# Operand tiles moved to new SBUF places, and the one-hot operations of the dense expert weights issued one by one, in a two-layer fp32 transformer block on one core

## The chip, the cores and the metric

The kernel runs on one core of one Trainium2 chip. The metric is the device time of one execution in microseconds; the figure of a kernel is the median of its runs, and a profiled execution has a time of its own. Times inside the trace are counted from the first instruction of the profiled execution.

## The reference, cut to what matters

Two transformer layers run one after the other on 256 tokens of width 1024, everything in float32. The first layer computes three mixers (windowed attention, a bidirectional linear recurrence, attention over a memory), gates and sums them, and adds a feed-forward layer over 16384 tiny experts (`peer_ffn`): each token picks 8 x 16 of them by a product-key top-k, and

```
act = gelu(einsum('chkd,cd->chk', u_tab[ix], hx))
out = einsum('chk,chkd->cd', gx * act, v_tab[ix])
```

The second stack has an attention layer with a SwiGLU feed-forward, then an attention layer with forget gates and a mixture of 8 SwiGLU experts of which each token takes two.

## The kernel before, in words

**Arithmetic.** Each float32 operand of a large product is split into a high part (rounded to the type `float32r`) and a low part (the rest). A product is three matmuls: high x high, high x low, low x high. `mm_fm` (line 377) streams 256 columns of an activation (`XH`, `XL`) past a 128 x 128 block of weights that sits in the array; `mm_tm` (line 382) streams 512 columns of weights past a 128 x 128 block of activations. So the activations are the moving operand in the first form and the stationary one, brought in by a weight load, in the second. All matmuls are issued at line 375.

**Weights.** `Stream` carries all weight tiles in order. SyncE loads a tile of 128 x 1024 float32 into a raw buffer (line 186), ScalarE writes its high part (line 200), VectorE its low part (line 211, called the low part below). There are three pairs of high and low tiles, more in some stages; when a tile is taken, `ahead` first issues the low parts that are waiting and then loads and splits as far as buffers allow. In the routing, the dense expert stage and what follows it `st.lag` is set: the low part of a tile is issued when the next tile is taken.

**The dense expert stages.** The tiny experts are computed densely. `u_phase(half)` multiplies all 128 groups of 128 experts by the tokens, one weight tile per half-step, and applies GELU (ScalarE, lines 1268 to 1272; VectorE multiplies by the gate weights where they are known, line 1273). `g_phase` makes the dense gate weights: for 8 tokens at a time, `prep` builds one-hot tiles on VectorE with four operations (two comparisons, lines 1303 and 1304, two products, line 1307), 16 half-precision matmuls multiply them into `pg`, and lines 1327 and 1329 multiply or copy the result into `act`. `weave` runs `g_phase` beside `u_phase(1)`: after each half-step of `u_phase` it takes 1.56 steps of `g_phase`, where a step ends at a `yield`. A group of 8 tokens has three steps: both comparisons; both products; the matmuls with line 1327. `v_phase` then multiplies by `peer_v` in the 512-column form.

**The last stage** runs the 8 experts: `in_mm` and `out_mm` use the 512-column form with the weight tiles moving and `XH`/`XL`/`X2`/`aH`/`aL` stationary. Raw buffers there number 24.

**Places in SBUF.** Tiles lie where their pools put them; pools are stacks, one from the left and one from the right, and `pad` (line 352) allocates unused bytes. Counting the tile sizes up in the order of the code gives each tile's first byte; its remainder modulo 512 is called its place here. All offsets inside these tiles are multiples of 512 bytes, so one place holds for every operand of a tile. Before the change the places are:

| tiles | role | place |
|---|---|---|
| weights `hwb`, `lwb` (3 pairs) and `hwx`, `lwx` | weights | 128 |
| `hwm`, `lwm` (output projection of layer 1) | weights | 0 |
| `hwc`, `lwc` | weights | 256 |
| `hwd`, `lwd` | weights | 384 |
| `XH`, `XL` | activations, mostly 256-column form | 192 |
| `YH`, `YL` (the same buffers 64 bytes lower or higher) | activations, 512-column form | 128, 256 |
| `catH`, `catL` | activations | 320 |
| `mgH`/`mgL`, `cH`/`cL` of the first attention of layer 2, `gh`/`glo`, `X2H`/`X2L`, `aH`/`aL` | activations, 512-column form | 0 |
| `mh2`, `ml2` | activations | 448 |
| `xnH`/`xnL`, `dm0` | gather of tokens | 128, 192 |

Of the kernel before, what the change touches and what calls it, by code (L numbers as in the profile page):

```python
# [7 lines left out]
F32 = mybir.dt.float32  # L8
FR = mybir.dt.float32r
# [258 lines left out]
def weave(main, *sides):  # L268

    sides = [[s[0], s[1], s[2] if len(s) > 2 else 0, 0.0] for s in sides]  # L270
    for n, _ in enumerate(main):
        for s in sides:
            if n < s[2]:
                continue
            s[3] += s[1]
            while s[3] >= 1.0 and s[0] is not None:
                s[3] -= 1.0
                if next(s[0], "end") == "end":
                    s[0] = None
# [37 lines left out]
def program(ctx, tc, A, out, dbg=None, stop=None, force=False):  # L317
# [11 lines left out]
    def pool(stack, name, bufs=1, side=None):  # L329
        kw = {} if side is None else {"side": side}  # L330
        return stack.enter_context(tc.tile_pool(name=name, bufs=bufs, reuse_waits="tile", **kw))
# [7 lines left out]
    def psum_b(n, name):  # L339

        bank_b.close()
        return bank_b.enter_context(tc.tile_pool(name=name, bufs=n, space=PSUM))

    psb = [psum_b(4, "psb")]
    resid = pool(ctx, "resid")
    small = pool(ctx, "small", 3)
    x1d = ctx.enter_context(tc.tile_pool(name="dram", bufs=1, space=bass.MemoryType.DRAM)).tile([128, 2, D], F32, name="x1d")
    ctx.enter_context(tc.manual_schedule())

    st = Stream(nc, strm, 5, 3)  # L350

    def pad(p, nbytes):

        p.tile([128, nbytes // 4], F32, name=f"pad{nbytes}_{len(pads)}")
        pads.append(nbytes)

    pads = []

    def pa():
        return psum.tile([128, 512], F32, name="pa")  # L360
# [13 lines left out]
    def mm(p, a, b, s, e):  # L374
        E.matmul(p, a, b, start=s, stop=e)  # L375
# [6 lines left out]
    def mm_tm(p, h, l, xh, xl, s, e):  # L382
        mm(p, xh, h, s, False)
        mm(p, xh, l, False, False)
        mm(p, xl, h, False, e)
# [9 lines left out]
    def split_to(h, l, src):  # L395
        T.activation(h, src, AF.Copy)  # L396
        V.tensor_sub(l, src, h.bitcast(F32))  # L397
# [85 lines left out]
                yield  # L483

    xt = resid.tile([128, 2, D], F32, name="xt")


    xbuf = [resid.tile([128, 2064], FR, name="X" + c) for c in "HL"]

    def shifted(*o):  # L490
        return [b[:, n:n + 2048].rearrange("p (k t) -> p k t", k=8) for b, n in zip(xbuf, o)]

    XH, XL = shifted(16, 0)
    YH, YL = shifted(0, 16)
    pad(resid, 64)
    phr = Pools()
    ctx.push(lambda *e: phr.close())
    misc = pool(phr, "pmisc", side="right").tile([128, 2048], F32, name="misc")
    HS = [slice(0, 512), slice(512, 1024)]
# [332 lines left out]
    for m in range(NF):  # L832
        st.add("ffn", A["w_ffn"], 3 * m, 3 * m + 2)
        if m >= LAG:
            q = m - LAG
# [30 lines left out]
    with Pools() as pha:  # L866
        pA = pool(pha, "pA")
# [4 lines left out]
        km = misc[:, 0:1024].rearrange("p (m t) -> p m t", m=4)  # L872
        vm = misc[:, 1024:2048].rearrange("p (a b) -> p a b", a=2)
        mt = misc.rearrange("p (a b) -> p a b", a=2)
        pad(pA, 64)
        catH = pA.tile([128, 16, 256], FR, name="catH")
        catL = pA.tile([128, 16, 256], FR, name="catL")
        mh, ml = catH[:, 8:16], catL[:, 8:16]
# [217 lines left out]
        phase_end("mix")  # L1096

        p1 = pool(pha, "p1m")
        pad(p1, 32)
        mgH = p1.tile([128, 8, 256], FR, name="mgH")  # L1100
        mgL = p1.tile([128, 8, 256], FR, name="mgL")
        st.extend(p1, 1, 2, st.end("wo"), "m")

        def proj(mp):
# [33 lines left out]
    act = [None, pool(ph1, "pR", side="right").tile([128, 64, 256], F32, name="act1")]  # L1138
# [119 lines left out]
    def u_phase(half):  # L1258
        blk = Blocks("u")
        for k in range(0, 64, 2):  # L1260
            p = pa()
            for i in range(2):
                fm_tile(p[:, i * 256:i * 256 + 256], blk, 8, XH, XL)
                if i == 0:
                    yield
            n, pv, to = seen["t"], p.rearrange("p (k t) -> p k t", k=2), act[half][:, k:k + 2]
            if n == 0:
                T.activation(to, pv, AF.Gelu_apprx_tanh)
            else:
                T.activation(pv[:, :, :n], pv[:, :, :n], AF.Gelu_apprx_tanh)  # L1270
                if n < 256:
                    T.activation(to[:, :, n:], pv[:, :, n:], AF.Gelu_apprx_tanh)
                V.tensor_mul(to[:, :, :n], pv[:, :, :n], to[:, :, :n])
            seen["k"] += 2
            yield
# [18 lines left out]
    def g_phase(ps):  # L1294

        def prep(n):
            a, c = oha[n % 2], ohc[n % 2]

            def pairs(x, i):
                return x[:, i, n * 8:n * 8 + 8].rearrange("p (u j) -> p u j", j=2)[:, :, None].to_broadcast([128, 4, 128, 2])  # L1300

            keys = io2[:, None].to_broadcast([128, 4, 128, 2])
            V.tensor_tensor(c[:, 0], keys, pairs(ib, 0), op=OP.is_equal)
            V.tensor_tensor(a, keys, pairs(ib, 1), op=OP.is_equal)
            yield
            for i in (1, 0):
                V.tensor_tensor(c[:, i], c[:, 0], pairs(gp, i), op=OP.mult)
            yield

        yield from prep(0)  # L1310
        for n in range(32):
            if n < 31:
                yield from prep(n + 1)
            a, c = oha[n % 2], ohc[n % 2]
            p = ps.tile([128, 1024], F32, name="pg")
            for i in range(8):
                u, j = i // 2, i % 2
                for q in range(2):
                    mm(p[:, i * 128:i * 128 + 128], a[:, u, :, j], c[:, q, u, :, j], q == 0, q == 1)
            pv = p.rearrange("p (t k) -> p k t", t=8)  # L1320
            ts, K = slice(n * 8, n * 8 + 8), seen["k"]
            for half in range(2):
                lo, hi = half * 64, half * 64 + 64
                m = min(max(K, lo), hi)
                if m > lo:
                    v = act[half][:, :m - lo, ts]
                    V.scalar_tensor_tensor(v, pv[:, lo:m], 2.0 ** -15, v, op0=OP.mult, op1=OP.mult)
                if m < hi:
                    T.activation(act[half][:, m - lo:, ts], pv[:, m:hi], AF.Copy, scale=2.0 ** -15)
            seen["t"] += 8  # L1330
            yield

    vacc = []

    def v_parts(half):

        done = set()

        def need(k):
            for q in (k, k + 1):  # L1340
                if q < 32 and q not in done:
                    done.add(q)
                    s = (q % 4) * 2
                    split_to(YH[:, s:s + 2], YL[:, s:s + 2], act[half][:, q * 2:q * 2 + 2])
        return need

    def v_phase(half, R, after):
# [21 lines left out]
    def v_mm(half, k, t, h, l, ns=(0, 1)):  # L1369
        ts = slice(t * 128, t * 128 + 128)  # L1370
        for n in ns:
            mm_tm(vacc[t][n], h[:, HS[n]], l[:, HS[n]], YH[:, k % 8, ts], YL[:, k % 8, ts],
                  half == 0 and k == 0, half == 1 and k == 63)

    g = g_phase(psum_b(2, "psg"))
    weave(u_phase(1), (g, 1.56))
    run(g)
    psb[0] = psum_b(4, "psb2")
    dump("act0", act[0])
# [1 line left out]
    run(v_phase(0, 0, None))  # L1381
    ph0.close()

    st.extend(pool(ctx, "strmc"), 2, 1, len(st.items), "c")
    phd = Pools()
    ctx.push(lambda *e: phd.close())
    c3_ = pool(phd, "c3")
    phs = Pools()
    ctx.push(lambda *e: phs.close())
    st.extend(pool(phs, "strmd"), 0, 2, st.end("kv1v"), "d")  # L1390
    phm = Pools()
    ctx.push(lambda *e: phm.close())
    pm2 = pool(phm, "pm2")
# [10 lines left out]
    permb = load_const(c3_, "permb")  # L1404
    sink2 = c3_.tile([128, 12], F32, name="sink2")
    nc.gpsimd.dma_start(sink2, rows(A["sink2"], 12))
    pad(pm2, 64)
    mh2 = pm2.tile([128, 8, 256], FR, name="mh2")
    ml2 = pm2.tile([128, 8, 256], FR, name="ml2")
    pad(pm2, 64)  # L1410
    m2 = misc.rearrange("p (k t) -> p k t", k=8)
    nc.gpsimd.dma_start(m2, A["mem2"])

# [21 lines left out]
    pr = pool(ctx, "pr", side="right")  # L1435
# [45 lines left out]
    with Pools() as ph:  # L1481
        p2 = pool(ph, "p2")
        t2 = pool(ph, "t2", 2)
# [38 lines left out]
        for h in range(12):  # L1522
            b = (h % 2) * 64
# [19 lines left out]
    with Pools() as ph:  # L1543
        p2 = pool(ph, "p2", 2)
# [9 lines left out]
        for m in range(NF):  # L1554
            p = pa()
# [7 lines left out]
            if m >= LAG:  # L1563
                h, l = st.take("ffn")
# [11 lines left out]
    with Pools() as ph:  # L1576
        p2 = pool(ph, "p2")
        t2 = pool(ph, "t2", 2)
# [68 lines left out]
        for h in range(12):  # L1647
            b = (h % 2) * 64
# [29 lines left out]
    Mk = pr.tile([128, 2, 8], F32, name="Mk")  # L1678
    Gt = pr.tile([128, 2, 8], F32, name="Gt")
    pos = pr.tile([128, 2, 8], F32, name="pos")  # L1680
    xnH = pr.tile([128, 2, D], FR, name="xnH")
    xnL = pr.tile([128, 2, D], FR, name="xnL")

    pen = pr.tile([128, 2, 8], F32, name="pen")
    dm0 = pr.tile([128, 2, 256], FR, name="dm0")

    def one_hot(dm, e, t, off=0, n=2):
        for i in range(n):
# [83 lines left out]
    with Pools() as ph:  # L1772
        p2 = pool(ph, "p2", side="right")
        t2 = pool(ph, "t2", 2, side="right")
        pad(t2, 32)
        st.extend(pool(ph, "strm3"), 7, 0, len(st.items), "f")
        st.load()
        x2 = [p2.tile([128, 8, 128], FR, name="X2" + c) for c in "HL"]
# [1 line left out]
        def rows_of(e, n=1):  # L1780

            if e % 3 == 2:
                return x2
            o = e % 3 * 128
            return [X[:, :, o:o + n * 128] for X in (YH, YL)]
        cnt = p2.tile([128, 1], F32, name="cnt")
        cni = p2.tile([128, 1], I32, name="cni")
        pad(p2, 64)

        def gather(p, ks, dm):  # L1790

# [202 lines left out]
        b = [small.tile([128, 2, 6], F32, name="bn") for _ in range(2)]  # L1994
        for t in range(2):
            for n in range(2):
                d = way[e][0][:, t * 128:t * 128 + 128]
# [31 lines left out]
```

## Time and profile before

| | |
|---|---|
| median of 3 runs | 2421.37 us (2420.82 to 2423.57) |
| profiled execution | 2422.57 us, of which the span of instructions is 2420.8 us |
| TensorE (PE) | busy 2352.5 us, 97% |
| VectorE (DVE) | busy 1862.3 us, 77% |
| ScalarE (ACT) | busy 1406.0 us, 58% |
| weights read | 528.55 MB on SyncE's queue |

PE is the matmul row and PEld the weight load row. Consecutive matmuls overlap in the records: one begins while the one before it is still passing through the array. So what a matmul costs in a row of matmuls is the distance from its start to the next start, called the pitch below, and not its recorded duration; the duration is the pitch and a constant part, which is why "mean ns of one" in a grouped row still tells the state of a group. The middle stretches run in this order: attention and recurrence to 306 us, routing and `u_phase(0)` to 556, `u_phase(1)` with `g_phase` to 778, `v_phase` to about 1142, the two attention layers and the SwiGLU layer (1264 to 1448) to about 1600, the experts to 2400.

### The profile page before, as it was taken

The numbers are of one execution on the slowest core, as the hardware profiler recorded it, in microseconds if no ns is written. First come the engines' busy times: TensorE is split into PE (matmuls) and PEld (weight loads), VectorE is DVE, ScalarE is ACT, GpSimd is POOL, SyncE is SP. The second block draws the span as 40 slices with busy tenths as digits, with TensorE's granted clock in tenths as the row PEclk, the third lists the DMA queues.
The fourth block names the chain that finished last, engine by engine and source line by source line (L and its number), as shares of the span: only waits on it lengthen the run. The fifth ranks groups of instructions, "written<-read, shape, count | busy, mean of one in ns | idle before, by whom it ended". The sixth has DMA issues, their size and how long they took to land. (4 is left out here: it accounts for less than half of the span.)

```text
span 2420.8 us, 37592 instructions
## 1 busy us (share of the span) xinstructions
PE 2352.5 (97%) x14264; PEld 2040.6 (84%) x14264; DVE 1862.3 (77%) x2825; ACT 1406.0 (58%) x1920; POOL 35.2 (1%) x48
## 2 busy tenths in 40 slices
PE   9999999999999999999999999989899999999997
PEld 8988999999898888888879997778788888888885
DVE  7776569798888555656685567589889989999997
ACT  5684444444444445544545444458677877877875
POOL 0100000000000000000000000000000000000000
PEclk9999999999999999999999999989999999999999
DMA  7335455554444557654426544379899999999992
GB/s 271 114 129 184 167 194 173 178 180 151 144 141 165 192 191 247 209 190 157 149 92 230 184 158 165 104 286 370 300 335 355 365 337 348 369 346 341 363 356 82
DMA packets 149646, 545.53 MB, mean 225 GB/s; under 512 B 16960, under 2 KB 17088, under 8 KB 148816
## 3 DMA queue, kind: packets, MB, share of 16 engines
q1 hardware_dynamic: 145728, 528.55, 61.8%
q0 software_dynamic: 2720, 10.50, 1.4%
q10 hardware_dynamic: 1008, 4.00, 0.4%
q8 instruction: 114, 1.87, 0.3%
q14 instruction: 76, 0.62, 0.1%
HBM read 540.88 MB, written 2.10 MB: 224 GB/s over the span
## 5 line engine op out<-in xcount | busy, mean ns | idle before, releaser
L211 DVE TENSOR_TENSOR lwb<-rawb,hwb 128x1024 fp32r<-128x1024 f32 (+1 forms) x406 | 494.0, 1225 | 92.9 <-ACT hwb L200 90.8
L200 ACT ACTIVATE hwb<-rawb 128x1024 fp32r<-128x1024 f32 (+1 forms) x406 | 426.8, 1056 | 214.5 <-PE pb L375 88.1
L375 PE MATMUL pa<-XH,lwb 128*128 128x256 f32 x1848 | 505.3, 281 | 16.8 <-DVE lwb L211 16.1
L375 PE MATMUL pa<-XH,hwb 128*128 128x256 f32 x1848 | 509.1, 283 | 0.4 <-ACT XH L511 0.2
L375 PE MATMUL pa<-XL,hwb 128*128 128x256 f32 x1848 | 501.4, 279 | 0.0
L375 PEld LDWEIGHTS pa<-XH,lwb 128*128 128x128 f32 x1848 | 340.1, 187 | 24.6 <-DVE lwb L211 24.5
L375 PEld LDWEIGHTS pa<-XH,hwb 128*128 128x128 f32 x1848 | 340.8, 188 | 4.4 <-issue 1.3
L375 PEld LDWEIGHTS pa<-XL,hwb 128*128 128x128 f32 x1848 | 340.6, 188 | 1.1
L211 DVE TENSOR_TENSOR lwb<-rawe,hwb 128x1024 fp32r<-128x1024 f32 x176 | 210.9, 1222 | 24.0 <-ACT hwb L200 19.4
L200 ACT ACTIVATE hwb<-rawe 128x1024 fp32r<-128x1024 f32 x176 | 185.8, 1059 | 25.4 <-PE pb L375 11.6
L211 DVE TENSOR_TENSOR lwb<-rawf,hwb 128x1024 fp32r<-128x1024 f32 x130 | 156.6, 1222 | 17.8 <-ACT hwb L200 13.7
L375 PE MATMUL pb<-hwb,XL 128*128 128x512 f32 (+1 forms) x428 | 165.5, 387 | 0.1
L375 PE MATMUL pb<-lwb,XH 128*128 128x512 f32 (+1 forms) x428 | 165.0, 386 | 0.0
L375 PE MATMUL pb<-hwb,XH 128*128 128x512 f32 (+1 forms) x428 | 163.4, 382 | 1.2 <-ACT XH L396 1.2
L375 PE MATMUL pa<-hwb,XH 128*128 128x512 f32 x396 | 159.0, 401 | 0.0
L375 PE MATMUL pa<-hwb,XL 128*128 128x512 f32 x396 | 156.8, 396 | 0.0
L375 PE MATMUL pa<-lwb,XH 128*128 128x512 f32 x396 | 156.2, 395 | 0.0
L200 ACT ACTIVATE hwb<-rawf 128x1024 fp32r<-128x1024 f32 x130 | 137.1, 1059 | 23.2 <-PE pa L375 11.3
L397 DVE TENSOR_TENSOR XL<-act,XH 128x512 fp32r<-128x512 f32 x64 | 44.1, 691 | 109.3 <-ACT XH L396 109.3
L375 PE MATMUL pb<-hwb,aH 128*128 128x512 f32 x264 | 104.5, 396 | 0.0
L375 PE MATMUL pb<-lwb,aH 128*128 128x512 f32 x264 | 104.0, 394 | 0.0
L375 PE MATMUL pb<-hwb,aL 128*128 128x512 f32 x264 | 104.0, 394 | 0.0
(611 smaller groups left out, 4918.3 us busy)
## 6 DMA issues: line engine op xcount, KB each, us to landing
rawe<-w_e SPq DMA_DIRECT2D x220, 512.0 KB, 5.3
rawf<-w_e SPq DMA_DIRECT2D x152, 512.0 KB, 5.2
rawb<-w_u SPq DMA_DIRECT2D x128, 512.0 KB, 3.5
rawb<-w_e SPq DMA_DIRECT2D x112, 512.0 KB, 5.3
rawb<-w_vt SPq DMA_DIRECT2D x110, 512.0 KB, 4.3
rawb<-w_ffn SPq DMA_DIRECT2D x47, 512.0 KB, 4.8
rawc<-w_e SPq DMA_DIRECT2D x44, 512.0 KB, 5.2
rawb<-w_mrg SPq DMA_DIRECT2D x36, 512.0 KB, 3.8
```

Source lines behind the costliest of these rows:

```text
L200: self.nc.scalar.activation(h[:, :n], r[:, :n], AF.Copy)
L211: self.nc.vector.tensor_sub(l[:, :n], r[:, :n], h[:, :n].bitcast(F32))
L375: E.matmul(p, a, b, start=s, stop=e)
L397: V.tensor_sub(l, src, h.bitcast(F32))
```

## The change

Two things. In `prep`, each of the four one-hot operations ends a step of its own (5 steps for 8 tokens instead of 3), and `weave` takes 2.6 steps after each half-step instead of 1.56. And tiles move: pads are added, changed or dropped, `small` is opened before `resid`, and `XH`/`XL` become plain tiles that serve both forms (`YH`/`YL` are gone).

```diff
     psb = [psum_b(4, "psb")]
+    small = pool(ctx, "small", 3)
     resid = pool(ctx, "resid")
-    small = pool(ctx, "small", 3)
...
-    xbuf = [resid.tile([128, 2064], FR, name="X" + c) for c in "HL"]
-
-    def shifted(*o):
-        return [b[:, n:n + 2048].rearrange("p (k t) -> p k t", k=8) for b, n in zip(xbuf, o)]
-
-    XH, XL = shifted(16, 0)
-    YH, YL = shifted(0, 16)
-    pad(resid, 64)
+    XH = resid.tile([128, 8, 256], FR, name="XH")
+    XL = resid.tile([128, 8, 256], FR, name="XL")
...
-        pad(pA, 64)
         catH = pA.tile([128, 16, 256], FR, name="catH")
...
-        pad(p1, 32)
+        pad(p1, 352)
         mgH = p1.tile([128, 8, 256], FR, name="mgH")
         mgL = p1.tile([128, 8, 256], FR, name="mgL")
+        pad(p1, 64)
         st.extend(p1, 1, 2, st.end("wo"), "m")
...
             V.tensor_tensor(c[:, 0], keys, pairs(ib, 0), op=OP.is_equal)
+            yield
             V.tensor_tensor(a, keys, pairs(ib, 1), op=OP.is_equal)
             yield
             for i in (1, 0):
                 V.tensor_tensor(c[:, i], c[:, 0], pairs(gp, i), op=OP.mult)
-            yield
+                yield
...
-                    split_to(YH[:, s:s + 2], YL[:, s:s + 2], act[half][:, q * 2:q * 2 + 2])
+                    split_to(XH[:, s:s + 2], XL[:, s:s + 2], act[half][:, q * 2:q * 2 + 2])
...
-            mm_tm(vacc[t][n], h[:, HS[n]], l[:, HS[n]], YH[:, k % 8, ts], YL[:, k % 8, ts],
+            mm_tm(vacc[t][n], h[:, HS[n]], l[:, HS[n]], XH[:, k % 8, ts], XL[:, k % 8, ts],
...
-    weave(u_phase(1), (g, 1.56))
+    weave(u_phase(1), (g, 2.6))
...
-    st.extend(pool(ctx, "strmc"), 2, 1, len(st.items), "c")
+    strmc = pool(ctx, "strmc")
+    pad(strmc, 64)
+    st.extend(strmc, 2, 1, len(st.items), "c")
...
-    st.extend(pool(phs, "strmd"), 0, 2, st.end("kv1v"), "d")
+    strmd = pool(phs, "strmd")
+    pad(strmd, 384)
+    st.extend(strmd, 0, 2, st.end("kv1v"), "d")
...
-    pad(pm2, 64)
+    pad(pm2, 448)
     mh2 = pm2.tile([128, 8, 256], FR, name="mh2")
     ml2 = pm2.tile([128, 8, 256], FR, name="ml2")
-    pad(pm2, 64)
...
+    dm0 = pr.tile([128, 2, 256], FR, name="dm0")
+    pen = pr.tile([128, 2, 8], F32, name="pen")
     xnH = pr.tile([128, 2, D], FR, name="xnH")
     xnL = pr.tile([128, 2, D], FR, name="xnL")
-
-    pen = pr.tile([128, 2, 8], F32, name="pen")
-    dm0 = pr.tile([128, 2, 256], FR, name="dm0")
...
-        pad(t2, 32)
...
-            return [X[:, :, o:o + n * 128] for X in (YH, YL)]
+            return [X[:, :, o:o + n * 128] for X in (XH, XL)]
...
-        pad(p2, 64)
```

Counted up in the same way, the places after the change are 128 for all weight tiles, 64 for `XH`/`XL`, `cat`, `mg`, `mh2`/`ml2`, the first `cH`/`cL`, `gh`/`glo`, `X2` and `aH`/`aL`, 128 for `dm0` and 192 for `xnH`/`xnL`.

## Rows read from the trace of the kernel before

**Rows 1.** The page's first part: busy time, share and instructions of each engine.

```profile
PE 2352.5 (97%) x14264; PEld 2040.6 (84%) x14264; DVE 1862.3 (77%) x2825; ACT 1406.0 (58%) x1920; POOL 35.2 (1%) x48
```

**Rows 2.** Busy time by stretch: PE, PEld, DVE, ACT, POOL, then clock, DMA share, GB/s.

```profile
300.00:556.00 256.00, 253.20 (x2125) 249.85 (x2124) 217.98 (x557) 120.88 (x143) 1.07 (x2) 1.00 0.53 178
556.00:778.00 222.00, 208.46 (x1963) 201.96 (x1961) 186.71 (x274) 91.31 (x151) 0.53 (x1) 1.00 0.44 147
...
1804.00:2004.00 200.00, 200.00 (x910) 162.85 (x909) 184.25 (x207) 157.72 (x191) 0.00 (x0) 1.00 0.97 351
```

**Rows 3.** One of the page's costliest groups: x count | busy us, mean ns | idle before it.

```profile
L375 PE MATMUL pa<-XH,lwb 128*128 128x256 f32 x1848 | 505.3, 281 | 16.8 <-DVE lwb L211 16.1
```

**Rows 4.** PE by instruction, u_phase(0): first and last of 48 pitches (start us, us).

```profile
380.04 0.28 PE L375 MATMUL pa<-XH,hwb 128*128 128x256 f32 x1
...
385.69 0.28 PE L375 MATMUL pa<-XH,hwb 128*128 128x256 f32 x1
```

**Rows 5.** PE by instruction, SwiGLU layer, weights `hwc`: first and last of 21 pitches.

```profile
1275.98 0.28 PE L375 MATMUL pa<-XH,hwc 128*128 128x256 f32 x1
...
1278.36 0.28 PE L375 MATMUL pa<-XH,hwc 128*128 128x256 f32 x1
```

**Rows 6.** PE by instruction, u_phase(1): a wait, then first and last of 18 pitches.

```profile
606.48 0.38 PE L375 MATMUL pa<-XH,lwb 128*128 128x256 f32 x1
606.70 0.28 PE L375 MATMUL pa<-XH,hwb 128*128 128x256 f32 x1
...
608.74 0.28 PE L375 MATMUL pa<-XH,hwb 128*128 128x256 f32 x1
```

**Rows 7.** PE by instruction, value projection of layer 1: first and last of 18 pitches.

```profile
64.23 0.28 PE L375 MATMUL pb<-hwb,XH 128*128 128x256 f32 x1
...
66.35 0.28 PE L375 MATMUL pb<-hwb,XH 128*128 128x256 f32 x1
```

**Rows 8.** PE groups of 46 to 57 us, memory values of layer 1, 512-column form.

```profile
L375 PE MATMUL pb<-lwb,catH 128*128 128x512 f32 x16 | 6.3, 392 | 0.0
L375 PE MATMUL pb<-hwb,catH 128*128 128x512 f32 x16 | 6.2, 388 | 0.0
L375 PE MATMUL pb<-hwb,catL 128*128 128x512 f32 x15 | 5.9, 394 | 0.0
```

**Rows 9.** PE groups of 778 to 1142 us, v_phase.

```profile
L375 PE MATMUL pb<-hwb,XL 128*128 128x512 f32 x384 | 152.5, 397 | 0.1
L375 PE MATMUL pb<-lwb,XH 128*128 128x512 f32 x384 | 152.1, 396 | 0.0
L375 PE MATMUL pb<-hwb,XH 128*128 128x512 f32 x384 | 149.5, 389 | 1.2 <-ACT XH L396 1.2
```

**Rows 10.** PE groups of 1760 to 2400 us, the experts.

```profile
L375 PE MATMUL pa<-hwb,XL 128*128 128x512 f32 x295 | 116.8, 396 | 0.0
...
L375 PE MATMUL pb<-hwb,aH 128*128 128x512 f32 x216 | 85.1, 394 | 0.0
...
L375 PE MATMUL pb<-hwb,aL 128*128 128x512 f32 x216 | 84.9, 393 | 0.0
```

**Rows 11.** PE group of 1264 to 1448 us, output product of the SwiGLU layer.

```profile
L375 PE MATMUL pb<-hwd,gh 128*128 128x512 f32 x76 | 30.0, 395 | 0.0
```

**Rows 12.** Groups of 556 to 778 us: PE's waits, then VectorE's operations.

```profile
L375 PE MATMUL pa<-XH,lwb 128*128 128x256 f32 x484 | 137.9, 285 | 13.5 <-DVE lwb L211 13.1
...
L211 DVE TENSOR_TENSOR lwb<-rawb,hwb 128x1024 fp32r<-128x1024 f32 x61 | 74.3, 1218 | 0.1
L1327 DVE SCALAR_TENSOR_TENSOR act<-pg,act 128x512 f32<-128x512 f32 x64 | 32.8, 554 | 3.9 <-PE pg L375 3.9
L1307 DVE TENSOR_TENSOR misc<-misc 128x1024 f16<-128x1024 f16 x30 | 20.6, 688 | 0.5
...
L1273 DVE TENSOR_TENSOR act<-pa,act 128x16 f32<-128x16 f32 (+28 forms) x29 | 12.3, 425 | 28.9 <-ACT act L1272 28.8
```

**Rows 13.** Busy time by stretch, end of the experts (columns as in rows 2).

```profile
2371.00:2400.00 29.00, 29.00 (x126) 22.92 (x125) 24.84 (x26) 20.89 (x25) 0.00 (x0) 1.00 0.01 3
```

More of the change, by code (lines that the diff above doesn't have):

```diff
@@ L350, in program @@
     st = Stream(nc, strm, 5, 3)
+    pads = []
     def pad(p, nbytes):
@@ L355, in pad @@
         pads.append(nbytes)
-    pads = []
     def pa():
```

## The prediction

> **What bounds the kernel now.** I read the busy times first: TensorE is busy 97% of the span, VectorE 77%, ScalarE 58% [rows 1]. By stretch, TensorE is full in u_phase(0) and in the experts and leaves 13.5 of 222 us in u_phase(1) [rows 2]. So nearly everywhere the end is set by how fast matmuls follow each other, and an idle gap is worth looking at in u_phase(1) alone. There the gaps are waits of the third matmul of a tile for the low part on VectorE, 13.1 us [rows 12].
>
> Then I read the pitch, instruction by instruction. The granted clock is 1.00 in these stretches [rows 2], the level of 2.4 GHz, at which 256 columns need 106.7 ns. In u_phase(0) 48 pitches take 5.65 us, 117.7 ns each [rows 4]. In the SwiGLU layer, same form and same 256 columns, 21 pitches take 2.38 us, 113.3 ns each [rows 5]. Nothing waits in either. What differs is where the operands lie. While a matmul streams, the weights of the next are loaded [both are matmuls with a load of their own in rows 1: 14264 of each]. Call d the place of the moving operand minus that of the operand loaded next. Rows 4 have `XH`/`XL` at 192 against weights at 128: d = +64. Rows 5 have weights at 256: d = -64.
>
> Two rows show that d alone does not fix the pitch. After a wait in u_phase(1), d = +64 runs at 113.3 ns (18 pitches in 2.04 us) until the tile ends [rows 6]; and in the value projection of layer 1, where weights at 128 move and `XH` at 192 is loaded, d = -64 runs at 117.8 ns (18 in 2.12 us) [rows 7]. So there are two states, a low and a high pitch, each kept until something interrupts; d shifts which one is reached. At +64 the low one is the exception: the mean record of the costliest group is 281 ns, where the stretch of rows 5 has 276 ns, and the page's 281 includes restarts.
>
> For 512 columns the recorded durations serve, being the pitch plus a constant. In v_phase the three products have 397, 396 and 389 ns, mean 394.0 [rows 9], with d = 0 (`YH` at 128) and -128 (`YL` at 256) mixed. In the experts, d = 0 or +-128, the groups that do not follow a transpose have 393 to 396, mean 394.3 [rows 10]; the SwiGLU output product, d = 128 or -128, has 395 [rows 11]. The lowest steady group is the memory values of layer 1: weights at 128, `cat` at 320, d = -192, with 388, 392 and 394, mean 391.3 [rows 8].
>
> **The change part by part.** After it, the 256-column form has d = 64 - 128 = -64 nearly everywhere, and the 512-column form has d = 128 - 64 = +64. The second attention's `cH`/`cL` keep their place against their weights. No instruction is added or taken away by the places; no load is moved, and no buffer is added, so SP's and POOL's queues keep their order.
>
> *Term 1, the 256-column form.* There are three groups like that of rows 3, 3 x 1848 = 5544 matmuls; 3 x 484 = 1452 of them lie in u_phase(1) [rows 12], 4092 elsewhere. Going from the high to the low state is worth 117.7 - 113.3 = 4.4 ns. At d = -64 both states occur [rows 5, 7]. I take 60% low, a little over half, since rows 5 got there from running matmuls, without a wait, and waits are rare outside u_phase(1) (16.8 us of idle before the whole group, 13.1 of it there [rows 3, 12]). That is 0.6 x 4.4 = 2.6 ns x 4092 = 10.6 us. Ends: 0 and 18.0 us.
>
> In u_phase(1) half of it is lost. Per half-step VectorE has a low part (1.22 us), 2.0 us of one-hot work (four operations of 0.688 and two of line 1327 at 0.554, 3.86 us per three steps, at 1.56 steps) and half of a line 1273 (0.21): 3.43 us. TensorE has 24 x 0.1177 = 2.82 us and the 16 matmuls of `pg`, in all 222 / 64 = 3.47 us with its waits [rows 2, 12]. VectorE is as full, so a faster TensorE finds it late: 1452 x 2.6 ns = 3.8 us, of which I take 1.9; ends 0 and 6.4.
>
> *Term 2, the 512-column form.* d = +64 has no row here. The nearest is d = -192 [rows 8], nearest because distances 256 apart look alike: d = 0 and 256 in the experts and d = 128 and -128 in rows 9 to 11 have durations within 3 ns of each other, and on the 256-column side no row contradicts it. I take 391.3. From the loops, the experts have 88 x 36 = 3168 such matmuls, v_phase 128 x 12 = 1536, the SwiGLU layer 22 x 12 = 264. That is 3168 x 3.0 + 1536 x 2.7 + 264 x 3.7 ns = 9.5 + 4.1 + 1.0 = 14.6 us. Ends: all at 389, the best row of rows 9, gives 26 us; all at 397, its worst, loses 8.6 + 4.6 + 0.5 = 13.7 us.
>
> The experts can give this back only if weights arrive as fast. The DMA share is 0.97 at 351 GB/s there [rows 2], near its ceiling; but the last load is over by 2371 us and TensorE works on to 2400 [rows 13]: some 29 us of weights lie loaded ahead. A gain of 9.5 us over 800 asks for 1.2% more, 355 GB/s, and the lead covers all of it once. Cover gone, the 9.5 us are lost.
>
> *Term 3, one-hot operations one by one.* VectorE runs in order; a low part issued with the next tile waits behind the steps that `weave` took. Before, 0.56 x 64 = 36 half-steps have two steps behind them, and a third of these, 12, are both comparisons and both products, 4 x 0.688 = 2.75 us. After, at most three steps lie there: two operations and the two of line 1327, 1.38 + 1.11 = 2.48 us. The latest low parts come 0.27 us sooner: 12 x 0.27 = 3.3 us of the 13.1. Steps per group and pace rise together (5 / 2.6 = 1.92 half-steps against 3 / 1.56 = 1.92), so `g_phase` ends where it did. The multiplication of line 1273, for which VectorE waits 28.8 us on ScalarE [rows 12], keeps its place in the queue: it is what is late next. Ends: 0 (the order behind that wait decides) and 13.1.
>
> **Sum.** 10.6 + 1.9 + 14.6 + 3.3 = 30.4 us. The profiled execution took 2422.57 us, 1.2 above the median of 2421.37; against the median it comes to **2391 us**.
>
> **The rivals.** *Places do not matter*, and the two pitches come from the states alone, entered by chance of timing. For it: rows 6 and 7 show either state at either d. Against it: rows 4 and 5 run long without waits at different pitches. Then term 3 alone is left: 2418 us, no change that can be told. The Trainium skill, TensorE: Matmul & The Clock Gate, Step-by-step: what each phase is for, says the same: two independent read ports, one for the streaming operand and one for weight loads, so that "Loading the next tile's weights doesn't steal SBUF read bandwidth from the running matmul". By that rule rows 4 and 5 should have one pitch; they have two.
>
> *The transfers take over in the experts*: a DMA share of 0.97 cannot follow and the lead runs dry. Then the 9.5 us go: 2400 us. Against it: 29 us of lead.
>
> *Slower: the 512-column form lands high at +64.* If 256 apart are not alike, +64 is a new distance; settling at 397 in the experts and v_phase costs 13.7 us, and should the 256-column form fall into its high state after each wait as in rows 7, only term 3 stands against it: 2421.4 + 13.7 - 3.3 = 2432 us. It decides from 395 ns on: 0.7 ns x 4968 is term 3. If only the 512-column half fails, terms 1 and 3 (15.8) meet 13.7: 2419 us, no change.
>
> **How the numbers follow.** A measurement of this kernel can tell about 0.2% (5 us) from no change. Forecast 0.75; transfers 0.08, also faster; places do not matter 0.08 and the half failure 0.04, both within 0.2%; slower 0.05. So faster 0.83, same 0.12, slower 0.05. Low end: term 1 all low, with half of it in u_phase(1) (18.0 + 3.2), term 2 at 390 ns (13.6 + 6.1 + 1.3), term 3 at 7: 49 us, 2372. High end: a third low (5.9 + 1.0), term 2 at 394 (1.2), term 3 at 1: 9 us, 2412. This range leaves out the three cases without a gain, 0.17.
>
> **What would show it.** In the grouped rows of after, `pa<-XH,lwb` should fall from 281 towards 278 ns, with long stretches at 276; in v_phase the three groups should draw together near 391, and the experts' groups come to 391 to 392. PE's wait for `lwb` in u_phase(1) should be near 10 us or above, at most the 13.1 now, the stretch some 5 us shorter. The experts should show no wait for a raw tile and a DMA rate near 355 GB/s. The prediction is wrong if the 256-column groups keep 279 to 281 outside u_phase(1), or if the experts' groups stay at 394 or rise: then distance was not the cause, or 256 apart are not alike.

## The result, and the profile of the kernel after

The kernel after takes 2396.2 us (median of 4 runs, 2394.71 to 2398.42); the kernel before took 2421.82 us in the 4 runs beside it (2420.82 to 2423.57). The ratio is 0.9894, with a 95% interval of 0.9877 to 0.9911: faster by 1.1%. The forecast was 2391 us, within 2372 to 2412. The profiled execution took 2396.9 us with a span of 2395.1, 25.7 us less than the span of before.

First the page's busy times of the kernel after (columns as in [rows 1]):

```profile
PE 2327.5 (97%) x14264; PEld 2025.3 (85%) x14264; DVE 1859.1 (78%) x2825; ACT 1406.0 (59%) x1920; POOL 35.2 (1%) x48
```

The same instructions run, and TensorE's share is still 97%. Its busy time fell by 25.0 us, about as much as the span: the gain is in the matmuls, not in idle time.

The busy time by stretch of the kernel after (columns as in [rows 2]): routing with u_phase(0), u_phase(1), a piece of the experts, and 25 us near their end:

```profile
302.00:552.00 250.00, 246.35 (x2119) 242.49 (x2117) 215.16 (x554) 120.28 (x141) 0.88 (x2) 1.00 0.58 183
552.00:770.00 218.00, 206.36 (x1956) 199.79 (x1954) 185.89 (x276) 92.72 (x154) 0.53 (x1) 1.00 0.48 152
...
1795.00:1995.00 200.00, 200.00 (x921) 164.50 (x920) 186.75 (x210) 159.68 (x195) 0.00 (x0) 1.00 0.98 356
...
2350.00:2375.00 25.00, 25.00 (x108) 19.51 (x107) 20.85 (x22) 17.55 (x21) 0.00 (x0) 1.00 0.00 1
```

In 200 us of the experts TensorE now does 921 matmuls where it did 910 [rows 2]. The DMA rate rose from 351 to 356 GB/s, and weights still lie ahead: nothing is loaded in the last stretch while TensorE is full.

Next, TensorE by instruction in u_phase(0), the first and last of 48 pitches (start us, us):

```profile
375.97 0.28 PE L375 MATMUL pa<-XH,hwb 128*128 128x256 f32 x1
...
381.41 0.28 PE L375 MATMUL pa<-XH,hwb 128*128 128x256 f32 x1
```

48 pitches take 5.44 us, 113.3 ns each, where [rows 4] had 117.7.

The grouped rows of the 512-column form: v_phase, then the output product of the SwiGLU layer, then the experts (columns as in [rows 9]):

```profile
L375 PE MATMUL pb<-lwb,XH 128*128 128x512 f32 x384 | 151.3, 394 | 0.0
L375 PE MATMUL pb<-hwb,XH 128*128 128x512 f32 x384 | 150.6, 392 | 1.2 <-ACT XH L396 1.2
L375 PE MATMUL pb<-hwb,XL 128*128 128x512 f32 x384 | 149.2, 388 | 0.1
...
L375 PE MATMUL pb<-hwd,glo 128*128 128x512 f32 x76 | 29.9, 394 | 0.0
L375 PE MATMUL pb<-lwd,gh 128*128 128x512 f32 x76 | 29.8, 392 | 0.0
L375 PE MATMUL pb<-hwd,gh 128*128 128x512 f32 x76 | 29.5, 388 | 0.0
...
L375 PE MATMUL pb<-hwb,aL 128*128 128x512 f32 x212 | 83.6, 394 | 0.0
L375 PE MATMUL pb<-lwb,aH 128*128 128x512 f32 x212 | 83.1, 392 | 0.0
L375 PE MATMUL pb<-hwb,aH 128*128 128x512 f32 x212 | 82.3, 388 | 0.0
```

All three stages have the three values 388, 392 and 394, mean 391.3: those of [rows 8], which were at d = -192 before. The matmuls of +64 behave as those of -192.

And u_phase(1), TensorE's wait and VectorE's groups (answering to [rows 12]; `prep`'s comparisons are lines 1295 and 1297 now, its products line 1300):

```profile
L375 PE MATMUL pa<-XH,lwb 128*128 128x256 f32 x481 | 137.0, 285 | 10.4 <-DVE lwb L211 10.3
...
L211 DVE TENSOR_TENSOR lwb<-rawb,hwb 128x1024 fp32r<-128x1024 f32 x60 | 73.0, 1216 | 0.1
...
L1265 DVE TENSOR_TENSOR act<-pa,act 128x16 f32<-128x16 f32 (+29 forms) x30 | 12.9, 430 | 29.3 <-ACT act L1264 27.1 <-ACT pa L1262 2.1
```

TensorE waits 10.3 us for low parts instead of 13.1, and VectorE waits on ScalarE at the gate multiplication almost as long as before, 27.1 us instead of 28.8.

By stage, from the start of its first matmul to that of the next stage. The mean pitch is over pairs of matmuls that follow without a wait (105 to 124 ns for 256 columns, 220 to 245 for 512); the low share is the part of the 256-column pitches of 115 ns or less.

| stage | length, us | 256 columns: ns, low share | 512 columns: ns |
|---|---|---|---|
| layer 1's mixers | 301.4 → 301.3 | 117.1, 0.15 → 116.1, 0.40 | 230.8 → 231.9 |
| routing, u_phase(0) | 255.6 → 250.9 | 117.7, 0.02 → 114.2, 0.80 | |
| u_phase(1) | 222.4 → 217.8 | 117.4, 0.09 → 116.1, 0.41 | |
| v_phase | 357.9 → 354.3 | | 231.3 → 228.9 |
| first attention of layer 2 | 149.6 → 149.1 | 115.7, 0.47 → 114.4, 0.76 | 232.0 → 229.5 |
| SwiGLU layer | 156.6 → 153.2 | 116.6, 0.29 → 113.9, 0.90 | 233.4 → 229.0 |
| second attention, routing | 158.5 → 158.4 | 116.0, 0.41 → 115.8, 0.48 | 230.6 → 229.8 |
| experts | 806.1 → 797.5 | (111 pitches) | 232.0 → 229.2 |

The lengths give 0.1 + 4.7 + 4.6 + 3.6 + 0.5 + 3.4 + 0.1 + 8.6 = 25.6 us, the whole of the gain.

One row needs care. The SwiGLU layer is counted here from its first output product; so the row of the first attention holds the first 28.6 us of the SwiGLU layer too (from 1258.3 us in the kernel before). That opening has a low share of 0.96 before and after; the attention by itself went from 0.19 to 0.64.

### The profile page after: what moved, and what is told of

Read it like the earlier page. It is cut to its first block, busy times and chain, and to the rows that moved or that the text cites. A ratio compares the mean times of both kernels' runs of the same rounds, so it can differ in the third digit from the quotient of the medians.

```text
span 2395.1 us, 37594 instructions
## 1 busy us (share of the span) xinstructions
PE 2327.5 (97%) x14264; PEld 2025.3 (85%) x14264; DVE 1859.1 (78%) x2825; ACT 1406.0 (59%) x1920; POOL 35.2 (1%) x48
## 5 line engine op out<-in xcount | busy, mean ns | idle before, releaser
L200 ACT ACTIVATE hwb<-rawe 128x1024 fp32r<-128x1024 f32 x176 | 185.6, 1058 | 24.4 <-PE pb L375 11.8
```

The costliest lines, as they stand in the source:

```text
L200: self.nc.scalar.activation(h[:, :n], r[:, :n], AF.Copy)
```

## The experiments

The theory: the pitch of a matmul depends on d, the place of its moving operand minus that of the operand loaded beside it, modulo 256; and, apart from that, the order of the one-hot operations shortens waits in u_phase(1). Rival 1: only the places modulo 512, or some tile's own place, matter. Rival 2: the places change how TensorE meets other engines or the DMAs in SBUF, and not TensorE alone. Rival 3: the states come by chance of timing.

**e1_deal: the one-hot operations alone.** The kernel before with this part of the change:

```diff
             V.tensor_tensor(c[:, 0], keys, pairs(ib, 0), op=OP.is_equal)
+            yield
             V.tensor_tensor(a, keys, pairs(ib, 1), op=OP.is_equal)
             yield
             for i in (1, 0):
                 V.tensor_tensor(c[:, i], c[:, 0], pairs(gp, i), op=OP.mult)
-            yield
+                yield
...
-    weave(u_phase(1), (g, 1.56))
+    weave(u_phase(1), (g, 2.6))
```

> The kernel before with the one-hot operations issued one by one (5 steps, 2.6 per half-step) and no tile moved. Theory (the places carry most of the gain): 3 us faster than before, about 2418.5 us, TensorE's wait for the low part in u_phase(1) near 10 us instead of 13.1, and the pitch of every stage as before (u_phase(0) 117.7 ns, v_phase 231 ns). Rival (places do not matter): the whole gain is here, about 2396 us.

Measured: 2417.99 us against 2422.1, ratio 0.9985 (0.9976 to 0.9994), 4.1 us. u_phase(1) went from 222.4 to 218.9 us at the old pitch (117.6 ns); the other stages kept theirs. The wait, in the grouped rows of u_phase(1):

```profile
L375 PE MATMUL pa<-XH,lwb 128*128 128x256 f32 x481 | 137.2, 285 | 9.7 <-DVE lwb L211 9.1
```

13.1 us of waits became 9.1, which is the 3.5 us of the stage and a little more. The step was put at 3.3.

**e2_places: the places alone.** The kernel after with `prep` and the pace 1.56 of the kernel before (the diff of e1 reversed).

> The kernel after with the one-hot operations issued in pairs as before (3 steps, 1.56 per half-step). Theory: about 2399 us, 3 us above the kernel after, all of it in u_phase(1); the pitches as in the kernel after (u_phase(0) near 114 ns, v_phase and experts 229 ns). Rival (places do not matter): about 2422 us.

Measured: 2397.75 us, ratio 0.9899 (0.9884 to 0.9914), 1.6 us above the kernel after where 3 was expected. u_phase(1) took 221.8 us, 0.6 less than before, with a low share of 0.30 and this row:

```profile
L375 PE MATMUL pa<-XH,lwb 128*128 128x256 f32 x481 | 137.2, 285 | 13.8 <-DVE lwb L211 13.2
```

So in u_phase(1) faster matmuls buy next to nothing as long as VectorE's order is the old one. v_phase (228.9 ns) and the experts (229.2 ns) are as in the kernel after. 24.4 us for the places and 4.1 for the order make 28.5, where both together gave 25.6; the runs of one kernel differ by 3 to 4.5 us, so whether the two parts simply add is not shown.

This run shows something else too. Up to routing it is the same program as the kernel after, and its first stage took 297.6 us with a low share of 0.78, where the kernel after had 301.3 us and 0.40. The state there is not fixed by the program up to there. Two more stages with the same places in both kernels show it. The opening of the SwiGLU layer is 0.96 low in the kernel after and 0.02 low in e2, one us longer. And the output projection of layer 1, 512 columns at d = +64, ran at 233 to 234 ns in the kernel after, which is why the 512-column figure of its first row rose, and at about 229 ns in e2. One of its groups in the kernel after, then in e2:

```profile
L375 PE MATMUL pb<-lwb,mgH 128*128 128x512 f32 x20 | 7.9, 397 | 0.0
...
L375 PE MATMUL pb<-lwb,mgH 128*128 128x512 f32 x20 | 7.8, 388 | 0.0
```

**e3_x320 and e4_x192: the place of the activations.** The kernel after, with a pad ahead of `XH` and the pads behind it made to leave all other places as they are:

```diff
+    pad(resid, 256)
     XH = resid.tile([128, 8, 256], FR, name="XH")
...
-        pad(p1, 352)
+        pad(p1, 96)
...
-    pad(strmc, 64)
+    pad(strmc, 320)
```

For e4 the three are 128, 224 and 448. In e3 `XH`/`XL` lie at 320 (d = 192 for 256 columns, -192 for 512), in e4 at 192 as before (d = 64 and -64); `cat` moves with them.

> The kernel after with XH, XL and cat at place 320 instead of 64, all else at its place: distance +192 instead of -64 in the 256-column form, -192 instead of +64 in the 512-column form. Theory (distances 256 apart are alike): within 4 us of the kernel after, 2396 us, with v_phase at 229 ns and u_phase(0) mostly in the low state. Rival (the place counts modulo 512, and only 64 against 128 is good): v_phase back at 231 to 233 ns, u_phase(0) at 116 to 118 ns, 2410 us or more.

> The kernel after with XH, XL and cat at place 192 instead of 64, all else at its place: distance +64 in the 256-column form and -64 in the 512-column form, the signs exchanged. Theory (the sign decides): u_phase(0) at 117.5 ns (6 us longer than after), v_phase at 232 to 233 ns (5 to 6 us longer), the experts that use XH 3 to 4 ns longer per matmul (6 us); some 2414 to 2420 us in all. Rival (the state is only a matter of restarts, or the gain comes from all operands of a kind having one place): within 4 us of 2396 us.

Measured: e3 2396.33 us, ratio 0.9890 (0.9875 to 0.9905); e4 2420.46 us, ratio 0.9990 (0.9981 to 0.9999). In e3 the large stages have the pitches of the kernel after: v_phase 228.90 ns in both, the experts 229.19 in both, u_phase(0) 114.6 with a low share of 0.71, the SwiGLU layer 0.90 low. Only the first stage (0.29 low) and the opening of the SwiGLU layer (0.02) differ, the two that differ in e2 as well. In e4 u_phase(0) is back at 117.5 ns (0.07 low), the SwiGLU layer has no low pitch left (0.00), and v_phase takes 233.3 ns and 361.0 us, longer than before the change. Its time lies just above the 2414 to 2420 us expected; as it keeps the new order, worth 4.1 us in e1, its places are no better than those of before. The grouped rows of v_phase in e4:

```profile
L375 PE MATMUL pb<-hwb,XH 128*128 128x512 f32 x384 | 152.0, 396 | 1.2 <-ACT XH L396 1.2
L375 PE MATMUL pb<-hwb,XL 128*128 128x512 f32 x384 | 152.0, 396 | 0.1
L375 PE MATMUL pb<-lwb,XH 128*128 128x512 f32 x384 | 151.9, 396 | 0.0
```

A place 256 bytes further changes nothing in the time and one 128 bytes further undoes the change, with the same program, loads and order: rival 1 in its form of modulo 512 and rival 3 as the whole story fall.

**e5_pitch: the pitch by itself.** One execution of TensorE alone, one float32r tile moving and another one loaded, in stretches of 48 matmuls of 256 columns or 24 of 512, six for each d. It leaves the whole computation out:

```diff
+    def stretch(ps, name, n, count, mo, so, read):
+        p = ps.tile([128, 512], F32, name=name)
+        for i in range(count):
+            m = mo + i % 8 * 512
+            s = so + i % 16 * 128
+            E.matmul(p[:, :n], sta[:, s:s + 128], mov[:, m:m + n], start=i == 0, stop=i == count - 1)
```

> A kernel that leaves the whole computation out: rows of matmuls alone, 256 columns (48 in a stretch) and 512 columns (24 in a stretch), moving operand and loaded operand at set places; six stretches for each distance, a wait of a different length ahead of each, distances -256 to +224 in steps of 32 with the loaded operand at place 128, and six distances again with it at 320. The tile names give columns, row (a or b), sign and distance. Theory (the distance modulo 256 sets the pitch, in two states for 256 columns): +64 and -192 give 229 ns for 512 columns (record 391 to 392), -64 and +192 233 to 234 (395 to 397), 0 and -256 228 to 231, +-128 232 to 233; for 256 columns -64 and +192 are low (record 276) in half or more of the stretches and +64 and -192 high (280) in nearly all; the rows with the other base give the same. Rival 1 (modulo 512): distances 256 apart differ by 2 ns or more. Rival 2 (the distance does not matter without other engines at work): one record for all distances.

Its timeline joins what follows without a gap in one row; the name holds columns, base (a or b, 192 bytes apart), sign (m is minus) and size of d. One stretch each:

```profile
967.71 4.72 PE L33 MATMUL n512ap0x<-mov,sta 128*128 128x512 f32 x20
...
1045.81 4.74 PE L33 MATMUL n512ap64x<-mov,sta 128*128 128x512 f32 x20
...
1202.73 5.06 PE L33 MATMUL n512ap192x<-mov,sta 128*128 128x512 f32 x21
...
251.74 3.68 PE L33 MATMUL n256am64x<-mov,sta 128*128 128x256 f32 x31
...
410.11 3.69 PE L33 MATMUL n256ap64x<-mov,sta 128*128 128x256 f32 x30
```

Less the last record, 4.72 - 0.39 us over 19 pitches is 227.9 ns for d = 0; in the same way 229 at +64, 233 at +192, and for 256 columns 113.3 at -64 and 117.6 at +64. The grouped rows add all six stretches of a d, first matmuls included:

```profile
L33 PE MATMUL n256ap0x<-mov,sta 128*128 128x256 f32 x288 | 36.0, 284 | 4.3 <-DVE got L35 4.3
...
L33 PE MATMUL n256ap64x<-mov,sta 128*128 128x256 f32 x288 | 35.4, 281 | 4.3 <-DVE got L35 4.3
L33 PE MATMUL n256am192x<-mov,sta 128*128 128x256 f32 x288 | 35.4, 281 | 4.3 <-DVE got L35 4.3
...
L33 PE MATMUL n512ap192x<-mov,sta 128*128 128x512 f32 x144 | 35.1, 399 | 4.3 <-DVE got L35 4.3
...
L33 PE MATMUL n512ap64x<-mov,sta 128*128 128x512 f32 x144 | 34.6, 396 | 4.3 <-DVE got L35 4.3
L33 PE MATMUL n512am192x<-mov,sta 128*128 128x512 f32 x144 | 34.6, 396 | 4.3 <-DVE got L35 4.3
...
L33 PE MATMUL n256am64x<-mov,sta 128*128 128x256 f32 x288 | 34.4, 279 | 4.3 <-DVE got L35 4.3
L33 PE MATMUL n512ap0x<-mov,sta 128*128 128x512 f32 x144 | 34.4, 394 | 4.3 <-DVE got L35 4.3
...
L33 PE MATMUL n256bm64x<-mov,sta 128*128 128x256 f32 x288 | 34.2, 278 | 4.3 <-DVE got L35 4.3
```

From the starts in all stretches (the last 16 pitches of each), with d taken modulo 256:

| d | 256 columns, ns | 512 columns, ns |
|---|---|---|
| 0 | 120.0 | 226.6 to 228.0 |
| 64 (and -192) | 117.8, one of six at +64 and base b 113.3 | 228.7 to 229.1, one stretch of six at each of the three 233.3 |
| 128 | 118.4 to 118.9, four of 24 at 120 | 232.0 to 232.3, seven of 24 at 233.3 |
| 192 (and -64) | 113.3, at -64 5 of 6 and at base b 6 of 6, at +192 3 and 5 of 6; the others 117.8 | 233.3 |

The other multiples of 32 lie between 116.6 and 120.2 for 256 columns and between 233.2 and 234.4 for 512. Distances 256 apart agree, and so do the two bases at one d but for the share of stretches in either pitch: rival 1 falls in both its forms. The other engines are idle during a stretch and no weights are loaded from memory: rival 2 falls, and the differences come from TensorE and its reads alone. That chance has a part is shown as well: at d = -64 a stretch of 256 columns takes one of two pitches and keeps it to its end, and so does one of 512 columns at d = +64.

The table says which d the kernel after left unused: 512 columns at d = 0.

**e6_d0: the 512-column form at d = 0.** A second view of the activations' buffers at place 128, used where they are loaded; the 256-column form stays at -64 (+192 for `XL`, 256 apart):

```diff
-    XH = resid.tile([128, 8, 256], FR, name="XH")
-    XL = resid.tile([128, 8, 256], FR, name="XL")
+    xbuf = [resid.tile([128, n], FR, name="X" + c) for n, c in ((2064, "H"), (2096, "L"))]
...
+    XH, XL = shifted(0, 48)
+    YH, YL = shifted(16, 0)
...
-            mm_tm(vacc[t][n], h[:, HS[n]], l[:, HS[n]], XH[:, k % 8, ts], XL[:, k % 8, ts],
+            mm_tm(vacc[t][n], h[:, HS[n]], l[:, HS[n]], YH[:, k % 8, ts], YL[:, k % 8, ts],
...
-            return [X[:, :, o:o + n * 128] for X in (XH, XL)]
+            return [X[:, :, o:o + n * 128] for X in (YH, YL)]
```

and pads that bring `mg`, the first `cH`/`cL`, `gh`/`glo`, `X2` and `aH`/`aL` from 64 to 128.

> The kernel after, with the operand loaded ahead of the 512-column form (activations) at place 128, the weights' own, so that d is 0, in the value projection, the experts, both SwiGLU output projections and the projections of the merged heads; the 256-column form keeps d = -64. Theory (the pitch follows d modulo 256, and is lowest at d = 0 for the 512-column form: 227.4 ns in the single measurement of the pitch, against 229.0 in the kernel after): value projection, first 512-column stage, from a mean pitch of 228.9 to 227.3 ns and from 354.3 to about 352 us; experts from 229.2 to 227.4 and from 797.5 to about 791 us; first SwiGLU output projection from 229.0 to 227.4; query scores and first low parts as after (114.2 ns in the mean). In all some 5,000 matmuls by 1.6 ns, 8 us: 2388 us, between 2385 and 2391. Rival A (the stages are held by something else, loads of weights or VectorE, once the matmuls pass 229 ns): the pitch falls but the experts stay within 2 us of 797.5, 2394 to 2397 us. Rival B (the shifted second view of the activations brings new waits, as buffers overlap): the value projection is longer than 354 us.

Measured: 2390.05 us (2388.99 to 2393.05) against 2422.11, ratio 0.9872 (0.9856 to 0.9889). v_phase fell to 226.7 ns and 350.9 us, the experts to 227.8 ns and 792.1 us (797.5 in the kernel after). The stretch of 200 us in the experts, and v_phase:

```profile
1785.00:1985.00 200.00, 200.00 (x925) 165.42 (x924) 187.97 (x210) 160.89 (x194) 0.00 (x0) 1.00 0.98 357
```

```profile
L375 PE MATMUL pb<-hwb,XH 128*128 128x512 f32 x384 | 149.5, 389 | 1.2 <-ACT XH L396 1.2
L375 PE MATMUL pb<-hwb,XL 128*128 128x512 f32 x384 | 149.5, 389 | 0.1
L375 PE MATMUL pb<-lwb,XH 128*128 128x512 f32 x384 | 149.4, 389 | 0.0
```

The loads keep up at 357 GB/s, so neither rival came. But one stage lost: the SwiGLU layer took 155.8 us instead of 153.2. Its 512-column form gained (389 ns), and its 256-column form, with its d unchanged, went to the high pitch throughout:

```profile
L375 PE MATMUL pa<-XL,hwb 128*128 128x256 f32 x201 | 56.5, 281 | 0.0
L375 PE MATMUL pa<-XH,lwb 128*128 128x256 f32 x201 | 56.5, 281 | 0.0
L375 PE MATMUL pa<-XH,hwb 128*128 128x256 f32 x200 | 56.2, 281 | 0.0
...
L375 PE MATMUL pb<-hwd,gh 128*128 128x512 f32 x76 | 29.6, 389 | 0.0
```

**e7_d0_gh64: the operand of that stage back at 64.** One pad less than in e6:

```diff
         p2 = pool(ph, "p2", 2)
-        pad(p2, 32)
         blk = Blocks("ffn")
```

> The kernel of e6_d0 with one tile kind moved back: the operand loaded in the first SwiGLU output projection (gh and glo) at place 64 again, so that its 512-column form has d = +64 as in the kernel after. In e6_d0 that stage took 155.8 us (kernel after: 153.2): its 512-column form fell to 226.8 ns, but the 256-column form that alternates with it never reached its low pitch (117.8 ns in the mean, 113.9 after). Theory (the state in which the 256-column form runs is set by the 512-column matmuls that it follows, and is then kept): the stage goes back to a low share near 0.9 and 153.2 us, every other stage as in e6_d0, 2387.5 us, between 2386 and 2389. Rival (the state in that stage is chance of the execution, or follows from other tiles that moved): the 256-column form stays at 117 ns or above there and the time at 2390.

Measured: 2387.87 us (2387.10 to 2388.83) against 2420.93, ratio 0.9860 (0.9844 to 0.9877). The stage is back at 153.2 us with a low share of 0.90 (0 in e6), and the other stages stayed within 1.4 us of e6:

```profile
L375 PE MATMUL pa<-XL,hwb 128*128 128x256 f32 x201 | 55.6, 277 | 0.0
L375 PE MATMUL pa<-XH,lwb 128*128 128x256 f32 x201 | 55.6, 276 | 0.0
L375 PE MATMUL pa<-XH,hwb 128*128 128x256 f32 x200 | 55.4, 277 | 0.0
L375 PE MATMUL pb<-hwd,glo 128*128 128x512 f32 x76 | 29.9, 394 | 0.0
```

So in this stage the state of the 256-column matmuls, at one and the same d = -64, follows from the 512-column ones ahead of them: after d = +64 they come to the low pitch, after d = 0 they don't. It isn't carried over from the opening of the layer: that is high (0.02 or 0.03 low) in e2, e3, e6 and e7 alike, and the stage comes to 0.90 in e2, e3 and e7 and stays at 0 in e6. Nor is d = +64 of the 512-column form enough: in e4, with the 256-column form at d = +64, the share is 0. This kernel is the fastest here, 33.1 us below before where the change had 25.6; all its runs lie below all of the kernel after, though the two were timed beside different runs of before.

## Why the prediction was right

**The bound.** That nearly every stage is set by the pitch held: TensorE's busy time and the span fell together, by 25.0 and 25.7 us.

**The reading of rows 4 and 5: right in the end, but by luck.** The prediction took the low pitch of [rows 5] for a mark of d = -64. Those rows lie in the opening of the SwiGLU layer, which in the kernel before ran at the low pitch with every weight tile, also with `hwb` (d = +64, as in [rows 4]) and `hwd` (d = -192); in e2, e3, e6 and e7 the same stretch is high, with d = -64 or +192 throughout. It shows a state that was kept; that the state belongs to d = -64 it doesn't show. The rest of the layer, where 512-column products come in between, would have shown it: there `hwb` is high (0.04 of the pitches low) and `hwc`, at d = -64, is low (0.94). The kernel before, 1258.5 to 1286.8 us, then 1286.8 to 1443:

```profile
L375 PE MATMUL pa<-XH,hwb 128*128 128x256 f32 x40 | 11.0, 276 | 0.0
L375 PE MATMUL pa<-XH,hwd 128*128 128x256 f32 x24 | 6.6, 276 | 0.0
...
L375 PE MATMUL pa<-XH,hwb 128*128 128x256 f32 x200 | 56.0, 280 | 0.0
...
L375 PE MATMUL pa<-XH,hwc 128*128 128x256 f32 x72 | 19.9, 276 | 0.0
```

**Term 1, 256 columns: pitches right, what they bring in time too large outside u_phase(1).** 10.6 us were forecast. The lengths of the stages without u_phase(1) give 0.1 + 4.7 + 0.5 + 0.1 and, in the SwiGLU layer, 3.4 less the 1.2 of its 512-column form: 7.6 us. Both pitches were right, 113.3 and 117.7 ns, and 60% low was a little under: of the term's 4092 matmuls 0.74 are low now and 0.08 were before, and their mean pitch fell by 2.9 ns where 2.6 was put. With the tiles that the term left out, the 5,470 or so 256-column pitches of these stages fell by 2.1 ns (0.18 to 0.66 low), 11.7 us. What was mis-sized is the step from pitch to time, which counted every nanosecond as gained because waits are rare there. In routing and u_phase(0) the pitches gave 6.9 us and the length 4.7: the faster TensorE came upon a late low part 13 times instead of 9 by the starts of the matmuls, and the pairs of 256-column matmuls more than 124 ns apart rose from 34 to 45. The group that waits, 300 to 556 us in the kernel before, then 302 to 552 in the kernel after:

```profile
L375 PE MATMUL pa<-XH,lwb 128*128 128x256 f32 x669 | 186.7, 281 | 2.2 <-DVE lwb L211 2.1
...
L375 PE MATMUL pa<-XH,lwb 128*128 128x256 f32 x671 | 186.5, 280 | 3.0 <-DVE lwb L211 2.5
```

The prediction named the mean record of this group as a sign, 281 towards 278 ns, and 279 to 281 as the sign of being wrong. It was a poor one, since the records at a wait are in the mean (up to 0.39 us); the two groups that don't wait fell there from 281 and 280 to 278 and 277, and the pitches decide. In the first stage the pitches gave 1.7 us and the length 0.1; this stage changes by some 4 us between executions (297.6 in e2), and why it does was not tried.

**Term 1 in u_phase(1) and term 3.** Together 1.9 + 3.3 = 5.2 us were forecast, and the stage is 4.6 us shorter. e1 gives 3.5 us to the order of the one-hot operations (4.1 of the whole time) and e2 0.6 to the places alone. So term 3 was right in size, though not in how it came: by the starts of the matmuls, waits over 0.8 us fell from 13 to 7 in e1 (7 in the kernel after, 13 in e2) and those of 0.4 to 0.6 us rose from 3 to 7. Some six waits lost half a microsecond each, where twelve were to lose 0.27; that the sums agree is luck. Of term 1 some 1 us is left in this stage where 1.9 was put: VectorE is as full as TensorE, as forecast, and TensorE finds it late. The waits came out at 10.3 us, between the 10 and 13.1 named, since a faster TensorE gains back part of e1's 9.1.

**Term 2, 512 columns: right.** The step that carried it took d = +64 as alike to -192, 391.3 ns. The groups have 388, 392 and 394, mean 391.3, and e5 measures 229 ns at both d. The reason given was weaker than the step: the rows named for it have d = 0, 256 and +-128 all within 3 ns, so they could not tell which distances are alike, and in e5 0 and 128 differ by 5 ns; e3 and e5 are what shows it. By pitches, the experts give 3168 x 2.79 ns = 8.8 us and the SwiGLU layer 264 x 4.4 = 1.2 (forecast 9.5 and 1.0), v_phase 1536 x 2.36 = 3.6 (4.1): 13.6 of 14.6. The three groups did not draw together, though; only their mean moved.

**Against its own time**, the sum of 30.4 us was 4.7 too large against the span: by the lengths, 3.0 in term 1 outside u_phase(1), 1.2 in term 2 and 0.6 in u_phase(1).

**The rivals.** *Places do not matter* falls by e4: the same program with `XH` at 192 has no gain from them left (0.9990). The Trainium skill, TensorE: Matmul & The Clock Gate, Step-by-step: what each phase is for, holds that loading the next weights takes no read bandwidth from the running matmul. The runs do not fit with that as it stands: 113.3 to 120 ns for the same 256 columns in e5, by the distance of the two operands alone. Chance of timing did keep a part: the openings and the first stage above. *The transfers take over* did not come: 356 GB/s, 357 in e6, and 25 us of lead left. *Slower* is real at another place: v_phase in e4 takes 361.0 us at d = -64, 3.1 more than before. At +64 it came in one small stage alone, the output projection of layer 1 in the kernel after (96 matmuls at 233 to 234 ns), as in 3 of 18 stretches of e5.

## What to carry to other kernels

Where TensorE is full, look at the distance between the starts of matmuls of one shape in different stages; if it differs without a wait, compare the places of the operands. Here, modulo 256 bytes, 512-column float32r matmuls were fastest with both operands at one place and 256-column ones with the moving operand 64 bytes below the loaded one; a tile that serves in both roles can have two views, with no instruction more (e6: 14264 matmuls, as before). Check every stage afterwards, since what one form does can set the state of the other. And a low pitch in one stretch is no proof of a good place: compare stretches that start afresh, several of them.

## What was not expected

- The best distance differs by form: d = 0 is lowest for 512 columns (227.4 ns) and among the highest for 256 (120 ns). Steps finer than 64 bytes matter too: at odd multiples of 32 no 512-column pitch was under 233.2 ns.
- The lower pitch of the 256-column form is a state, not a rate: 0 or 0.90 of the pitches in the same stage by the place of another form's operand (e6, e7), and 0.40 or 0.78 in the first stage with the same program up to there (the kernel after, e2). The 512-column form has two states at d = +64 as well (about 229 and 233.3 ns). What sets a state at a start is open.
- Mixed distances are not a mean. In v_phase before, two of three loads had d = 0 and one -128; e5's 227.4 and 232.2 ns would give 229.0, and the stage had 231.3.
- What inside TensorE or its reads of SBUF makes the pitch depend on d was not shown by any run; e5 only excludes other engines and loads from memory.
